# Seven block products of eight in the feed-forward's first product and in six of eight gated units of a conformer, with two accumulators in tiles of their own

## Chip, cores and metric

The kernel runs on one core of one Trainium2 chip. The metric is the device time of one execution in microseconds (us). All inputs and outputs are in HBM; the kernel starts with nothing on chip.

## The reference, cut to what matters

One residual block over 16 learned positions and 512 frames (T = 528), model width 1024, in float32. `hybrid_layer` reads, in short:

```
u = rmsnorm(h, norm_mix_w);  proj = u @ w_in                 # 1024 x 8208
c_val, c_gate, q, k, v, z, a_dt, b_beta, gate_logits = split(proj)
c = c_val * sigmoid(c_gate)                                   # the gated unit, 1024 channels
c = silu(layernorm(causal_dwconv(c, 31 taps)));  y_conf = c @ w_conf_out
o = gated delta rule over q, k, v (8 heads of 128, chunks);  y_dn = (rmsnorm(o) * silu(z)) @ w_dn_out
h = h + (sigmoid(gA) * y_conf + sigmoid(gB) * y_dn) @ w_out
up = causal_dwconv(rmsnorm(h, norm_ffn_w) @ w_up, 3 taps)     # 1024 x 5632: the feed-forward's first product
f_gate, f_val = split(up);  h = h + (silu(f_gate) * f_val) @ w_down
out = rmsnorm(h, norm_final_w), the 512 frames
```

## The kernel before

Activations lie transposed: 128 channels on the partitions, time along the free dimension, so a width of 1024 is 8 tiles. Every large product is made of three partial ones, because each operand is held as two float32r tiles, hi (the rounded value) and lo (what was left): hi times hi, hi times lo and lo times hi are added in PSUM. `weights` loads a 128 x 1024 block of a weight matrix on the SP queue into a tile `wr` (3 slots), ScalarE casts it to `wh` and VectorE subtracts to `wl` (2 slots each). `gemm` then issues, for one output tile of 128 channels, 8 blocks of the contraction x 3 parts x 2 halves of the time axis = 48 matmuls. The order of the parts is PARTS: the two with `wh` first, the one with `wl` last.

`glu(f)` (eight times) makes tile f of the gated unit from two such products, `cg` and `cv`, of 264 columns a matmul: tanh of half the gate on ScalarE, one VectorE instruction for the product, then the 31 taps of the depthwise convolution, 30 of them VectorE instructions into `ca`, which are given a late priority (+20000). Between and behind them come the keys, the heads of the delta rule (`heads`), the gates, the layer norm of `ca` and the three products behind it. `up(t)` (44 times) makes one tile of the feed-forward's first product, 258 columns a matmul, from the residual `hs` times its norm weight, as `hh` and `hl`; the factor of the second norm, `r2v`, is multiplied in when `up` takes the result out of PSUM, so that the products need not wait for it. Three taps follow (one on ScalarE, two on VectorE), Silu of the gate tile, the product of both, and a split into `fh`, `fl`. Then come 8 output tiles of the down product, `dn`, and the final norm.

Nothing is executed in the order of the source. `record` writes all instructions down with a priority, and `Plan.order` puts each engine's instructions into a fixed order by simulating the engines with costs of its own (`price`, `LAT`, RATE) and priorities shifted by BIAS, IVP, LNP and the like. On the chip each engine then runs its list in that order and waits on semaphores. SBUF tiles come from pools of fixed size: `bt` (128 x 532 float32) has 75 slots, which nearly all activations share, `iv` 3. In PSUM `p2` has 2 slots of two banks and `p1` 4 slots of one bank. All instructions are emitted by one line, so the profile's line is L459 nearly everywhere; groups are told apart by tile names.

POOL's queue holds the memsets of the first columns of `ra` (the padding that q, k and v are convolved with), eight `affine_select` for the decay tiles `E`, and four memsets of `LL`. All DMAs are issued on SP's queue.

## Time and profile before

| what | us |
|---|---|
| runs, median of 3 (lowest to highest) | 1035.56 (1034.06 to 1035.69) |
| the profiled execution's own time | 1031.66 |
| span of its trace, first to last instruction | 1029.9 |
| TensorE busy | 1015.1 |
| VectorE busy | 717.1 |
| ScalarE busy | 473.6 |
| GpSimd busy | 9.4 |

The profiled execution is one run; its own time is the span and 1.8 us around it. It lies 3.9 us below the median of the three runs. Busy times are of instructions on the engine; waits and DMA issues are not in them.

### The profile page before, as it was taken

The numbers are of one execution on the slowest core, as the hardware profiler recorded it, in microseconds if no ns is written. First come the engines' busy times: TensorE is split into PE (matmuls) and PEld (weight loads), VectorE is DVE, ScalarE is ACT, GpSimd is POOL, SyncE is SP. The second block draws the span as 40 slices with busy tenths as digits, with TensorE's granted clock in tenths as the row PEclk, the third lists the DMA queues.
The fourth block names the chain that finished last, engine by engine and source line by source line (L and its number), as shares of the span: only waits on it lengthen the run. The fifth ranks groups of instructions, "written<-read, shape, count | busy, mean of one in ns | idle before, by whom it ended". The sixth has DMA issues, their size and how long they took to land.

```text
span 1029.9 us, 20012 instructions
## 1 busy us (share of the span) xinstructions
PE 1015.1 (99%) x8430; PEld 973.8 (95%) x8430; DVE 717.1 (70%) x1237; ACT 473.6 (46%) x844; POOL 9.4 (1%) x45
## 2 busy tenths in 40 slices
PE   9998999999999999999999999999999999999996
PEld 7998999998999999999999999999999999988886
DVE  5987999999999999443565555666676767622334
ACT  6777713468545545444373334544434443422222
POOL 0000000000000000000000000000000000000000
PEclk9999999998999999999999999999999999999999
DMA  6243423241212133123214333222232222233332
GB/s 229 76 115 82 128 90 114 83 103 64 73 63 82 53 114 115 62 73 114 93 43 154 128 109 100 85 83 100 86 99 88 86 99 87 93 93 92 97 92 82
DMA packets 44042, 98.40 MB, mean 96 GB/s; under 512 B 12720, under 2 KB 19248, under 8 KB 43952
## 3 DMA queue, kind: packets, MB, share of 16 engines
q1 hardware_dynamic: 43952, 97.12, 29.5%
q8 instruction: 66, 1.08, 0.4%
q14 instruction: 24, 0.20, 0.1%
HBM read 93.89 MB, written 3.21 MB: 94 GB/s over the span
## 4 chain that ended last, share of the span: by engine, by line
PE 93%; DVE 4%; ACT 1%; DMA 1%; issue 0%; SPq 0%; DVEq 0%; ACTq 0%
PE up L459 25%; PE dn L459 12%; PE ga L459 9%; PE y L459 9%; PE q L459 5%; PE v L459 5%; PE z L459 5%; PE wo L459 5%; PE cv L459 4%; PE cg L459 4%; PE o L459 2%; DVE cv L459 1%; PE k L459 1%; PE rs L459 1%; PE S L459 1%; PE qk L459 1%
## 5 line engine op out<-in xcount | busy, mean ns | idle before, releaser
L459 DVE TENSOR_TENSOR wl<-wr,wh 128x1024 fp32r<-128x1024 f32 x157 | 189.2, 1206 | 154.3 <-PE dn L459 59.8
L459 ACT CAST wh<-wr 128x1024 fp32r<-128x1024 f32 x157 | 162.2, 1035 | 257.1 <-PE dn L459 58.2
L459 DVE SCALAR_TENSOR_TENSOR ca<-c,par,ca 128x516 f32<-128x516 f32 (+12 forms) x240 | 176.7, 745 | 3.7 <-ACT ca L459 1.0
L459 PE MATMUL up<-hl,wh 128*128 128x258 f32 x704 | 141.5, 282 | 0.0
L459 PE MATMUL up<-hh,wh 128*128 128x258 f32 x704 | 141.5, 282 | 0.0
L459 PEld LDWEIGHTS up<-hh,wh 128*128 128x128 f32 x704 | 109.2, 190 | 0.2 <-issue 0.2
L459 PEld LDWEIGHTS up<-hl,wh 128*128 128x128 f32 x704 | 108.7, 189 | 0.0
L459 PE MATMUL up<-hh,wl 128*128 128x258 f32 x704 | 92.3, 284 | 0.0
L459 PEld LDWEIGHTS up<-hh,wl 128*128 128x128 f32 x704 | 88.2, 190 | 0.0
L459 PE MATMUL dn<-fh,wh 128*128 128x512 f32 (+1 forms) x198 | 71.6, 370 | 0.0
L459 PE MATMUL dn<-fl,wh 128*128 128x512 f32 (+1 forms) x198 | 71.6, 370 | 0.0
L459 DVE SCALAR_TENSOR_TENSOR uy<-up,par,uy 128x512 f32<-128x512 f32 x88 | 65.9, 749 | 2.8 <-ACT uy L459 1.3
L459 DVE TENSOR_TENSOR up<-up,r 128x258 f32<-128x258 f32 x88 | 33.5, 420 | 47.4 <-PE up L459 44.6
L459 ACT ACTIVATE uy<-up,par 128x512 f32<-128x512 f32 x44 | 35.9, 817 | 55.8 <-DVE up L459 55.8
L459 PE MATMUL ga<-ul,wh 128*128 128x258 f32 (+1 forms) x256 | 58.0, 288 | 0.0
L459 PE MATMUL ga<-uh,wh 128*128 128x258 f32 (+1 forms) x256 | 57.2, 288 | 0.0
L459 DVE SCALAR_TENSOR_TENSOR cv<-ra,par,cv 128x528 f32<-128x528 f32 x69 | 51.7, 765 | 1.4 <-ACT cv L459 1.3
L459 PE MATMUL dn<-fh,wl 128*128 128x512 f32 (+1 forms) x198 | 45.4, 369 | 0.0
L459 PEld LDWEIGHTS dn<-fh,wh 128*128 128x128 f32 x198 | 37.2, 188 | 7.0
L459 PEld LDWEIGHTS dn<-fl,wh 128*128 128x128 f32 x198 | 37.2, 188 | 6.9
L459 PE MATMUL ga<-uh,wl 128*128 128x258 f32 (+1 forms) x256 | 43.1, 286 | 0.0
L459 PEld LDWEIGHTS ga<-ul,wh 128*128 128x128 f32 x256 | 42.2, 190 | 0.6 <-issue 0.4
(284 smaller groups left out, 2194.6 us busy)
## 6 DMA issues: line engine op xcount, KB each, us to landing
wr<-in_win SPq DMA_DIRECT2D x64, 512.0 KB, 3.4
wr<-in_wup SPq DMA_DIRECT2D x44, 512.0 KB, 3.4
wr<-in_wd SPq DMA_DIRECT2D x17, 512.0 KB, 3.5
wr<-in_wdn SPq DMA_DIRECT2D x8, 512.0 KB, 3.5
wr<-in_wco SPq DMA_DIRECT2D x8, 512.0 KB
wr<-in_wo SPq DMA_DIRECT2D x8, 512.0 KB, 3.4
wr<-in_wd SPq DMA_DIRECT2D x8, 384.0 KB, 3.5
x<-in_xT SPq DMA_DIRECT2D x8, 264.0 KB, 5.6
```

The costliest lines, as they stand in the source:

```text
L459: getattr(engines[o.eng], o.fn)(*(get(x) for x in o.a), **{n: get(x) for n, x in o.k.items()})
```

## The change

The first product of the feed-forward is taken in pairs, a gate tile with its value tile (22 pairs). The first NPRE = 3 pairs stay as they were. The other 19, and six of the eight gated units (all but the first NGLU = 2), become products of 2 x 2 blocks: the contraction is cut into even and odd tiles of 128, the output into the two tiles of the pair, and the time axis into its two halves. Seven block products (12 matmuls each: 4 blocks of the contraction x 3 parts) replace eight.

- `seven` runs the seven products into two PSUM tiles of one bank, X and Z, of pool `p1`, by turns X, Z, X, Z, X, Z, X. A product in X or Z goes on adding to what is there, and `use` reads the running sum after each product: four times on ScalarE (copy, or times -1), three times on VectorE (added to or subtracted from the copy in SBUF). `quarters` says which quarter of the two result tiles each reading goes to.
- The weights need seven blocks of 128 x 512 for a pair: three are plain, four are sums or differences. `presums` makes these four ahead, in DRAM, with DMAs issued on POOL's queue that add while they copy: five DMAs for a pair, those for the gated units after the load of x, those for the feed-forward after the last `affine_select`. Each group also waits for the one two before it. `seven` then calls `weights` four times, three times for 1024 columns and once for 512.
- The activations need seven blocks too. `ufactors` makes them for the gated units from `us`, once for each two tiles of the contraction; `factors` does it for the feed-forward, from the normalised residual, which `second_norm` now computes itself (16 instructions).
- For the 19 pairs the norm's factor is no longer multiplied in when PSUM is read. The taps are split off as `taps3` and `ends`, under a priority of their own.
- The residual tiles `hs` are written to DRAM (`d_h`) and read back tile by tile in the down product (`back`). `fh`, `fl` of the last three pairs go to slots of pool `iv`.
- The 32 diagonal copies into `Mn` move from ScalarE to POOL.
- The order's constants change (RATE, STAY, SWITCH, IVP, `tail`, a price for DMAs of POOL, and the table BIAS, which is left out below).

```diff
-RATE = 0.4453
+RATE = 0.4475
...
-STAY = 1500
-SWITCH = 300
...
+STAY = 7500
+SWITCH = 480
...
-IVP = 1265
+IVP = 765
...
+NGLU = 2
+NPRE = 3
...
-        o.tail = 950 + (2800 if fn == "dma_start" and o.lat > 700 and self.run(k) <= P else 0)
+        o.tail = 1300 + (5000 if fn == "dma_start" and o.lat > 700 and self.run(k) <= P else 0)
...
+            if eng == "POOL":
+                return 1000, int(np.prod(out.shape)) * 4 / 122.0
...
+                dma = max(dma, t + 1350) + o.lat * (1.5 if soft > t else 1)
                 o.end = dma + o.tail
+            elif o.fn == "dma_start":
+                soft = max(soft, t + 2000) + o.lat
...
+    def presums(src, n, hold):
+        r = [plan.tile("dram", "con", [P, 4, HD], F32, "ws") for _ in range(n)]
+        for m in range(n):
+          with plan.at(1):
+            h = {hold} | ({softs[-2]} if len(softs) > 1 else set())
+            plan.after = set(h)
+            G.dma_start(out=r[m][:, 0:2], in_=src[:, m, 0:3:2])
+            plan.after = set(h)
+            G.dma_start(out=r[m][:, 2:4], in_=src[:, m, 0:2])
+            G.dma_start(out=r[m][:, 1:3], in_=src[:, m, 3:4].broadcast_to([P, 2, HD]), accum_op=ALU.add)
+            G.dma_start(out=r[m][:, 0], in_=r[m][:, 1], accum_op=ALU.add)
+            G.dma_start(out=r[m][:, 3], in_=r[m][:, 0], accum_op=ALU.add)
+            softs.append(len(plan.ops) - 1)
+        return r
...
+    def seven(src, m, sums, B, w, use):
+        X, Z = p1("sx")[:, :w], p1("sz")[:, :w]
+        flat = lambda v: v.rearrange("p b c -> p (b c)")
+        tiles = (flat(src[:, m, 0:2]), flat(sums[m][:, 0:2]), flat(sums[m][:, 2:4]), src[:, m, 2])
+        for i, (b, to, first, what) in enumerate((('b11', X, True, 'p1'), ('b21', Z, True, 'c11b'),
+                                                  ('t2', X, False, 'u2'), ('t1', Z, True, 'c22b'),
+                                                  ('t3', X, False, 'u3'), ('b22', Z, False, 'c12b'),
+                                                  ('t4', X, False, 'c21'))):
+            if i % 2 == 0:
+                with plan.at("sw"):
+                    hi, lo = weights(tiles[i // 2], D if i < 6 else HD)
+            n, c = len(B), i % 2 * HD
+            runs = [(k, x, y) for part in PARTS for k in range(n) for x, y in ((lo, 0), (hi, 0), (hi, 1))[part]]
+            for j, (k, x, y) in enumerate(runs):
+                PE.matmul(to, lhsT=x[:, c + k * P:c + (k + 1) * P], rhs=B[k][b][y], start=first and j == 0, stop=j == len(runs) - 1,
+                          skip_group_check=not first)
+            use(what, to)
...
+    def quarters(src, m, sums, B, w, n):
+        c = [bt(n=n), bt(n=n)]
+        q = lambda i, j: c[i][:, j * w:(j + 1) * w]
+        def use(what, acc):
+            i, j = {'p1': (0, 0), 'u2': (0, 1), 'c22b': (1, 1), 'c21': (1, 0),
+                    'c11b': (0, 0), 'c12b': (0, 1), 'u3': (1, 1)}[what]
+            if what in ('p1', 'u2'):
+                S.copy(out=q(i, j), in_=acc)
+            elif what in ('c22b', 'c21'):
+                S.mul(out=q(i, j), in_=acc, mul=-1.0)
+            else:
+                V.tensor_tensor(out=q(i, j), in0=q(i, j), in1=acc, op=ALU.subtract if i else ALU.add)
+        seven(src, m, sums, B, w, use)
+        return c
...
+    def factors(x0, x1, w, n, hold=None):
+        q = 2 * (w + 2)
+        sub = lambda t: t[:, :q].rearrange("p (b w) -> p b w", b=2)[:, :, :w]
+        two = lambda t: t[:, :2 * w].rearrange("p (b w) -> p b w", b=2)
+        t = bt(n=n + "t")
+        X0, X1, TT = two(x0), two(x1), two(t)
+        hold = set() if hold is None else {hold}
+        plan.after = set(hold)
+        V.tensor_tensor(out=TT[:, 0], in0=X0[:, 0], in1=X0[:, 1], op=ALU.subtract)
+        V.tensor_tensor(out=X0[:, 1], in0=X1[:, 1], in1=X0[:, 1], op=ALU.subtract)
+        V.scalar_tensor_tensor(out=TT[:, 1], in0=TT[:, 0], scalar=-1.0, in1=X1[:, 1], op0=ALU.mult, op1=ALU.subtract)
+        t4 = bt(n=n + "q")
+        V.scalar_tensor_tensor(out=t4[:, :w], in0=TT[:, 1], scalar=-1.0, in1=X1[:, 0], op0=ALU.mult, op1=ALU.subtract)
+        r = {}
+        for v, names in ((X0, ('b11', 't3')), (X1, ('b21', 'b22')), (TT, ('t1', 't2'))):
+            hi, lo = bt(F32R, n + "h"), bt(F32R, n + "l")
+            plan.after = set(hold)
+            S.copy(out=sub(hi), in_=v)
+            V.tensor_tensor(out=sub(lo), in0=v, in1=sub(hi.bitcast(F32)), op=ALU.subtract)
+            for b, nm in enumerate(names):
+                r[nm] = (sub(hi)[:, b], sub(lo)[:, b])
+        hl = bt(F32R, n + "hl")
+        S.copy(out=sub(hl)[:, 0], in_=t4[:, :w])
+        V.tensor_tensor(out=sub(hl)[:, 1], in0=t4[:, :w], in1=sub(hl.bitcast(F32))[:, 0], op=ALU.subtract)
+        r['t4'] = (sub(hl)[:, 0], sub(hl)[:, 1])
...
+    def ufactors(k):
+        two = lambda t: t[:, :T].rearrange("p (b w) -> p b w", b=2)
+        X0, X1 = two(us[k]), two(us[k + 1])
+        t, q = bt(n="ut"), bt(n="uq")
+        TT, QQ = two(t), two(q)
+        V.tensor_tensor(out=TT[:, 0], in0=X0[:, 0], in1=X0[:, 1], op=ALU.subtract)
+        V.tensor_tensor(out=QQ[:, 0], in0=X1[:, 1], in1=X0[:, 1], op=ALU.subtract)
+        V.scalar_tensor_tensor(out=TT[:, 1], in0=TT[:, 0], scalar=-1.0, in1=X1[:, 1], op0=ALU.mult, op1=ALU.subtract)
+        V.scalar_tensor_tensor(out=QQ[:, 1], in0=TT[:, 1], scalar=-1.0, in1=X1[:, 0], op0=ALU.mult, op1=ALU.subtract)
+        r = {}
+        for v, names in ((t, ('t1', 't2')), (q, ('t3', 't4'))):
+            hi, lo = split(v[:, :T], T, "uf")
+            for b, nm in enumerate(names):
+                r[nm] = (two(hi)[:, b], two(lo)[:, b])
+        for nm, j, b in (('b11', 0, 0), ('b21', 1, 0), ('b22', 1, 1)):
+            c = slice(PAD + 264 * b, PAD + 264 * (b + 1))
+            r[nm] = (uh[k + j][:, c], ul[k + j][:, c])
+        return r
...
+    wgs, uf = presums(A['wgq'], KT - NGLU, max(j for x in xh for _, j, w in x.tl.hist if w)), []
...
-                S.copy(out=Mn[h][r, :, r], in_=D8(h)[r])
+                G.tensor_copy(out=Mn[h][r, :, r], in_=D8(h)[r])
...
+        if f < NGLU:
+            acc = p2("cg")
+            gemm(acc, weights(A['win'][8 + f]), uh, ul, FULL)
+            t = bt(n="ct")
+            S.activation(out=halves(t[:, :T], 264), in_=acc[:, :, :264], func=AF.Tanh, scale=0.5)
+            acc = p2("cv")
+            gemm(acc, weights(A['win'][f]), uh, ul, FULL)
+            c = bt(n="c")
+            V.scalar_tensor_tensor(out=halves(c[:, :T], 264), in0=halves(t[:, :T], 264), scalar=1.0, in1=acc[:, :, :264],
+                                   op0=ALU.add, op1=ALU.mult)
+        else:
+            t, c = quarters(A['wgq'], f - NGLU, wgs, uf, 264, "c")
+            S.activation(out=t[:, :T], in_=t[:, :T], func=AF.Tanh, scale=0.5)
+            V.scalar_tensor_tensor(out=c[:, :T], in0=t[:, :T], scalar=1.0, in1=c[:, :T], op0=ALU.add, op1=ALU.mult)
...
+    for k in range(0, KT, 2):
+        with plan.at("gf"):
+            uf.append(ufactors(k))
...
+    wus = presums(A['wuq'], FT - NPRE, masks[-1])
...
+    d_h = [con([P, SEQ], "d_h", "dram") for _ in range(KT)]
+    for f in range(KT):
+        SY.dma_start(out=d_h[f], in_=hs[f][:, 4:TW])
...
+        for f in range(0, KT, 2):
+            with plan.at(f"h{f}"):
+                ab = []
+                for i in range(2):
+                    x = bt(n="xn")
+                    for b in range(2):
+                        V.scalar_tensor_tensor(out=x[:, b * 258:(b + 1) * 258], in0=hs[f + i][:, 2 + 256 * b:260 + 256 * b],
+                                               scalar=pc('nf', f + i), in1=r2v[b], op0=ALU.mult, op1=ALU.mult)
+                    ab.append(x)
+                ub.append(factors(*ab, 258, "n"))
...
+    def ffn(t):
+        if t < NPRE:
+            g, v = up(t), up(NPRE + t)
+        else:
+            g, v = quarters(A['wuq'], t - NPRE, wus, ub, 258, "up")
+        with plan.at("tp" if t < NPRE else "tq"):
+            ends(t, g, v)
+    def ends(t, g, v):
+        g = taps3(g, t)
         S.activation(out=g[:, :SEQ], in_=g[:, :SEQ], func=AF.Silu)
-        v = up(FT + t)
+        v = taps3(v, FT + t)
         V.tensor_tensor(out=g[:, :SEQ], in0=g[:, :SEQ], in1=v[:, :SEQ], op=ALU.mult)
-        a, b = split(g[:, :SEQ], SEQ, "f")
+        if t < FT - 3:
+            a, b = split(g[:, :SEQ], SEQ, "f")
+        else:
+            hl = plan.tile("sb", "iv", [P, D], F32R, "fv")
+            a, b = hl[:, :SEQ], hl[:, SEQ:]
+            S.copy(out=a, in_=g[:, :SEQ])
+            V.tensor_tensor(out=b, in0=g[:, :SEQ], in1=a.bitcast(F32), op=ALU.subtract)
         fh.append(a)
         fl.append(b)
+    for t in range(FT):
+        call(ffn, "u", t)
...
+    def back(f):
+        o = bt(n="hr")
+        SY.dma_start(out=o[:, 4:TW], in_=d_h[f])
+        hr.append(o)
+        return o
...
-        o = hs[f]
+        o = back(f)
...
+def _quarters(w):
+    k, n = w.shape
+    v = w.reshape(k // 256, 2, P, n // 256, 2, P).transpose(2, 3, 4, 1, 0, 5)
+    v = np.stack([v[:, :, 0, 0], v[:, :, 0, 1], v[:, :, 1, 1], v[:, :, 1, 0]], 2)
+    return np.ascontiguousarray(v).reshape(P, n // 256, 4, k // 2)
...
+    glu = np.stack([w[:, D:2 * D].reshape(D, KT, P), w[:, :D].reshape(D, KT, P)], 2)
+    a['wgq'] = _quarters(glu[:, NGLU:].reshape(D, -1))
...
+    w = w_up[0].reshape(D, 2, FT, P)
+    a['wup'] = _pack(w[:, :, :NPRE].reshape(D, -1))
+    a['wuq'] = _quarters(w[:, :, NPRE:].transpose(0, 2, 1, 3).reshape(D, -1))
+    a['wd'] = _pack(w_down[0])
```

## Rows read from the trace of the kernel before

**Rows 1.** The page: span, busy time by engine, VectorE's busy tenths in 40 slices.

```profile
span 1029.9 us, 20012 instructions
PE 1015.1 (99%) x8430; PEld 973.8 (95%) x8430; DVE 717.1 (70%) x1237; ACT 473.6 (46%) x844; POOL 9.4 (1%) x45
...
DVE  5987999999999999443565555666676767622334
```

**Rows 2.** The chain that ended last, shares of the span by engine.

```profile
PE 93%; DVE 4%; ACT 1%; DMA 1%; issue 0%; SPq 0%; DVEq 0%; ACTq 0%
```

**Rows 3.** Windows: length, busy us (instructions) by engine, clock, DMA share, GB/s.

```profile
70.00:180.00 110.00, 106.53 (x869) 104.08 (x868) 101.18 (x264) 56.52 (x160) 6.16 (x10) 1.00 0.38 112
180.00:425.00 245.00, 244.18 (x2352) 236.80 (x2351) 228.26 (x370) 133.62 (x287) 2.29 (x18) 0.99 0.26 81
425.00:640.00 215.00, 214.94 (x1890) 212.16 (x1890) 112.15 (x149) 90.59 (x135) 0.00 (x0) 1.00 0.30 100
...
640.00:674.40 34.40, 34.40 (x292) 34.04 (x291) 23.05 (x34) 16.78 (x22) 0.00 (x0) 1.00 0.26 85
...
725.00:875.00 150.00, 150.00 (x1253) 150.00 (x1252) 103.06 (x157) 62.02 (x78) 0.00 (x0) 1.00 0.28 92
...
894.80:1018.00 123.20, 123.20 (x615) 102.20 (x614) 42.72 (x53) 35.43 (x43) 0.00 (x0) 1.00 0.29 86
```

**Rows 4.** The chain in order of time: start us, us, what.

```profile
127.73 5.85 PE cv L459 x48
...
639.82 5.97 PE up L459 x49
...
650.35 244.47 PE up L459 x2037
...
894.82 115.13 PE dn L459 x528
```

**Rows 5.** Groups of instructions in 675:875: busy us, mean ns, idle before.

```profile
L459 DVE SCALAR_TENSOR_TENSOR uy<-up,par,uy 128x512 f32<-128x512 f32 x70 | 52.4, 749 | 1.2
L459 DVE TENSOR_TENSOR wl<-wr,wh 128x1024 fp32r<-128x1024 f32 x35 | 42.5, 1215 | 0.0
L459 ACT CAST wh<-wr 128x1024 fp32r<-128x1024 f32 x35 | 36.4, 1039 | 38.3 <-PE up L459 38.3
L459 ACT ACTIVATE uy<-up,par 128x512 f32<-128x512 f32 x35 | 28.6, 817 | 47.8 <-DVE up L459 47.8
L459 DVE TENSOR_TENSOR up<-up,r 128x258 f32<-128x258 f32 x70 | 26.5, 420 | 38.0 <-PE up L459 38.0
L459 DVE TENSOR_TENSOR fl<-uy,fh 128x512 fp32r<-128x512 f32 x17 | 11.8, 692 | 23.7 <-ACT fh L459 23.7
```

**Rows 6.** ScalarE and VectorE in order of time where the second norm's factor arrives.

```profile
649.94 0.82 ACT L459 COPY r<-rc 128x258 f32<-128x258 f32 x2 [3.27 <-PE rc L459]
...
650.80 0.76 DVE L459 TENSOR_TENSOR up<-up,r 128x258 f32<-128x258 f32 x2 [2.81 <-ACT r L459]
```

**Rows 7.** Tile `ca`: durations (min/median/max ns), first and last start.

```profile
L459 DVE SCALAR_TENSOR_TENSOR ca<-c,par,ca x240: 706/746/1147, 95.0 to 412.0; 128x516 f32<-128x516 f32 x46, 128x515 f32<-128x515 f32 x8, 128x513 f32<-128x513 f32 x8, 128x511 f32<-128x511 f32 x8
...
L459 DVE TENSOR_TENSOR ca<-ca,mean x8: 687/690/695, 517.3 to 521.6; 128x516 f32<-128x516 f32 x8
```

**Rows 8.** POOL and VectorE in order of time: start us, us, what [idle before].

```profile
71.83 1.11 POOL L459 TENSOR_SCALAR_AFFINE_SELECT E<-E 128x512 f32<-128x512 f32 x1 [64.31 <-DMA E<-d_g]
...
75.11 0.63 POOL L459 TENSOR_SCALAR_AFFINE_SELECT E<-E 128x512 f32<-128x512 f32 x1 [2.17 <-DMA E<-d_g]
...
113.11 0.14 POOL L459 MEMSET ra<- 128x4 f32 x2
...
397.92 0.17 POOL L459 MEMSET ra<- 128x4 f32 x3 [41.30 <-ACT v L459]
...
72.36 1.13 DVE L459 SCALAR_TENSOR_TENSOR cv<-ra,par,cv 128x528 f32<-128x528 f32 x1
```

**Rows 9.** DMA: the queue with its share of 16 engines; issues with median us to landing.

```profile
q1 hardware_dynamic: 43952, 97.12, 29.5%
...
wr<-in_wup SPq DMA_DIRECT2D x44, 512.0 KB, 3.4
...
x<-in_xT SPq DMA_DIRECT2D x8, 264.0 KB, 5.6
```

More of the change, by code (lines that the diff above doesn't have):

```diff
@@ L37 @@
 ROW = T + PAD
+HD = D // 2
 _COLS = [('mix', 8), ('cw', 8 * KCONF), ('cb', 8), ('lw', 8), ('lb', 8), ('dw', 24 * 4), ('bg', 16),
@@ L63, in __init__ @@
         self.row = int(np.prod(shape[1:]))
-        self.hist, self.first, self.real, self.left = [], None, None, 0
+        self.hist, self.first, self.real, self.left, self.serial = [], None, None, 0, plan.count
 class Vw:
@@ L242, in at @@
         was = self.late
-        self.prio, self.late = self.prio + by, was or late and by > 0
+        self.prio, self.late = self.prio + by, was or late
         yield
@@ L333, in order @@
         for v in {v for o in ops for v in o.tiles if v.tag in KEEP}:
-            heapq.heappush(line[v.tag], (v.first, id(v), v))
-        table, dma, low, done = None, 0.0, 0, bytearray(len(ops))
+            heapq.heappush(line[v.tag], (v.first, v.serial, v))
+        table, dma, soft, low, done = None, 0.0, 0.0, 0, bytearray(len(ops))
         array = Array()
@@ L420, in order @@
             if e == "SP":
-                dma = max(dma, t + 1350) + o.lat
+                dma = max(dma, t + 1350) + o.lat * (1.5 if soft > t else 1)
                 o.end = dma + o.tail
+            elif o.fn == "dma_start":
+                soft = max(soft, t + 2000) + o.lat
+                o.end = soft + 1500
             out.append(i)
@@ new lines, in ufactors @@
+    def ufactors(k):
[15 more added lines that the diff above has]
+            r[nm] = (uh[k + j][:, c], ul[k + j][:, c])
+        return r
@@ L642, in record @@
     raw = [out_raw(acc) for acc in raw]
+    softs = []
+    wgs, uf = presums(A['wgq'], KT - NGLU, max(j for x in xh for _, j, w in x.tl.hist if w)), []
     us = []
@@ L797, in decays @@
                         compare_op=ALU.is_ge, fill=-1e30)
+        masks.append(len(plan.ops) - 1)
         for n in range(NC):
@@ L845, in grams @@
             SY.dma_start(out=d_m[b, h].rearrange("n j t -> j n t"), in_=mn[32 * b:32 * b + 32, :, 32 * b:32 * b + 32])
+    masks = []
     ivt = {}
@@ L959, in glu @@
     def glu(f):
-        acc = p2("cg")
-        gemm(acc, weights(A['win'][8 + f]), uh, ul, FULL)
-        t = bt(n="ct")
-        S.activation(out=halves(t[:, :T], 264), in_=acc[:, :, :264], func=AF.Tanh, scale=0.5)
-        acc = p2("cv")
-        gemm(acc, weights(A['win'][f]), uh, ul, FULL)
-        c = bt(n="c")
-        V.scalar_tensor_tensor(out=halves(c[:, :T], 264), in0=halves(t[:, :T], 264), scalar=1.0, in1=acc[:, :, :264],
-                               op0=ALU.add, op1=ALU.mult)
+        if f < NGLU:
[12 more added lines that the diff above has]
+            V.scalar_tensor_tensor(out=c[:, :T], in0=t[:, :T], scalar=1.0, in1=c[:, :T], op0=ALU.add, op1=ALU.mult)
         a = bt(n="ca")
@@ L1197, in record @@
         sq = s
-    r2v = []
+    d_h = [con([P, SEQ], "d_h", "dram") for _ in range(KT)]
+    for f in range(KT):
+        SY.dma_start(out=d_h[f], in_=hs[f][:, 4:TW])
+    r2v, ub = [], []
     def second_norm():
@@ L1212, in up, with taps3 @@
         u = bt(n="up")
+        for b in range(2):
+            V.tensor_tensor(out=u[:, b * 258:(b + 1) * 258], in0=acc[:, b, :258], in1=r2v[b], op=ALU.mult)
+        return u
+    def taps3(u, t):
         uv = halves(u[:, :516], 258)
-        for b in range(2):
-            V.tensor_tensor(out=uv[:, b], in0=acc[:, b, :258], in1=r2v[b], op=ALU.mult)
         y = bt(n="uy")
@@ L1224, in record @@
     fh, fl = [], []
-    for t in range(FT):
-        g = up(t)
+    def ffn(t):
[7 more added lines that the diff above has]
+        g = taps3(g, t)
         S.activation(out=g[:, :SEQ], in_=g[:, :SEQ], func=AF.Silu)
-        v = up(FT + t)
+        v = taps3(v, FT + t)
         V.tensor_tensor(out=g[:, :SEQ], in0=g[:, :SEQ], in1=v[:, :SEQ], op=ALU.mult)
-        a, b = split(g[:, :SEQ], SEQ, "f")
+        if t < FT - 3:
[5 more added lines that the diff above has]
+            V.tensor_tensor(out=b, in0=g[:, :SEQ], in1=a.bitcast(F32), op=ALU.subtract)
         fh.append(a)
         fl.append(b)
+    for t in range(FT):
+        call(ffn, "u", t)
     cuts = ((0, 8), (8, 8), (16, 6))
+    hr = []
+    def back(f):
[3 more added lines that the diff above has]
+        return o
     def wdown(f, i):
@@ L1253, in record @@
     f, hw, ws = KT - 1, SEQ // 2, {}
-    o, s = hs[f], bt(n="fsq")
+    o, s = back(f), bt(n="fsq")
     for b in range(2):
@@ L1272, in record @@
             for j in range(2):
-                V.tensor_tensor(out=y[:, j], in0=hs[i + j][:, ch], in1=rb[:, :hw], op=ALU.mult)
+                V.tensor_tensor(out=y[:, j], in0=hr[i + j][:, ch], in1=rb[:, :hw], op=ALU.mult)
             SY.dma_start(out=out[i:i + 2, :, c].rearrange("f p t -> p f t"), in_=y)
@@ L1320, in arrays @@
     a['wco'], a['wdn'], a['wo'] = _pack(w_conf_out[0]), _pack(w_dn_out[0]), _pack(w_out[0])
-    a['wup'], a['wd'] = _pack(w_up[0]), _pack(w_down[0])
+    w = w_up[0].reshape(D, 2, FT, P)
+    a['wup'] = _pack(w[:, :, :NPRE].reshape(D, -1))
+    a['wuq'] = _quarters(w[:, :, NPRE:].transpose(0, 2, 1, 3).reshape(D, -1))
+    a['wd'] = _pack(w_down[0])
     taps = lambda v: v.reshape(v.shape[0], -1, P).transpose(2, 1, 0).reshape(P, -1)
```

2 lines of the change are left out of this document (1 added, 1 removed).

## The prediction, as put on record before the result

> **What bounds the kernel now.** I read the page first: TensorE is busy for 1015.1 of 1029.9 us, VectorE for 70%, ScalarE for 46%, GpSimd for 1% [rows 1]. A busy TensorE alone proves nothing, so the chain of waits came next: 93% of it is TensorE, 4% VectorE, 1% each ScalarE and DMA [rows 2]. Then the windows by stage [rows 3]: from 425 us to the end of the down product TensorE never rests. From 70 to 425 it loses 3.5 and 0.8 us, and there VectorE is nearly full too: 101.2 of 110, then 228.3 of 245. So fewer matmuls shorten the kernel wherever something else does not take their place, and the reader is to see which engine has how much room: in the feed-forward VectorE is 103.1 of 150 us busy, ScalarE 62.0.
>
> **What it removes.** A pair of feed-forward tiles takes 96 matmuls of 258 columns; seven products of 12 take 84. In the chain 2037 such matmuls last 244.47 us, 120.0 ns each [rows 4], so a pair goes from 11.52 to 10.08 us. 19 pairs x 12 x 0.120 = 27.4 us. A gated unit has 264 columns, 48 matmuls in 5.85 us or 121.9 ns [rows 4]: 6 x 12 x 0.1219 = 8.8 us. Together 36.2 us of TensorE's time. Each matmul already has a weight load of its own (8430 and 8430, [rows 1]), so that each block product meets new weights changes nothing.
>
> **What it adds on VectorE and ScalarE in the feed-forward.** Now a pair is 2 weight subtractions of 1.215, 4 readings of PSUM at 0.420, 4 taps at 0.749 and 2 of 0.692 (the product of gate and value taken as the split): 8.49 us by duration [rows 5]. The window has 103.06 us in 150/11.52 = 13.0 pairs, 7.92 each [rows 3]; instructions back to back overlap a little, factor 0.933. After: 3.5 subtractions and 3 readings, so 8.49 + 1.82 - 0.42 = 9.89, times 0.933 = 9.2 of 10.08 us, 92%. ScalarE has 62.02/13.0 = 4.8 us; it gains 1.5 casts of 1.039 and 4 readings, as the 258-column copy, whose two take 0.82 together with their overlap [rows 6], or 0.41 each: 4.8 + 1.6 + 1.6 = 8.0, 79%. Both still fit, VectorE only just. What it cannot do in time are taps, which nothing reads before the down product.
>
> **Waits that it adds.** X may not be written before its running sum has been read. While it is read the product in Z runs, 12 x 0.120 = 1.44 us; the reading is 0.41 or 0.42. It is late only when its engine has just begun something long: 1.215 + 0.42 is 0.2 us over 1.44. Five such waits in a pair, 25 pairs. Bounds: nothing, or 125 x 0.2 = 25 us. I take one wait in six, 4 us, because VectorE is full at 92% but the order puts the reading by its priority.
>
> **Weights.** A pair needs 3.5 tiles, one in 2.88 us instead of 5.76. A `wr` slot is held for landing, cast and subtraction, 3.4 + 1.04 + 1.22 + an issue of 0.3 = 6.0 us [rows 5, 9]; three slots give one in 2.0 us. Even the slowest landing in the rows, 5.6 us, gives 2.7. In the two `wh`, `wl` slots a tile has 2.88 us for 1.04 + 1.22 = 2.26. Hidden, with 0.6 us to spare; if that is gone it shows as a wait behind ScalarE or VectorE, counted above. The load in the feed-forward rises from 92 GB/s, 0.28 of the DMA engines [rows 3], to 1.835 MB in 10.08 us, 182 GB/s and about 0.55. The 16 transfers of `d_h` carry 4 MB beside 97 [rows 9] and are read one tile per 15 us of down product; nothing.
>
> **Entry to the feed-forward.** The first product starts at 639.8 [rows 4] and the norm's factor is there at 650.8 [rows 6]. Three plain pairs last 34.6 us, so 23.6 are left for 16 normalising instructions and four calls of `factors` (each 4 of half width, 3 at full width and one more of half width). By the nearest rows, 0.42 and 0.69, that is 6.7 + 8.4 + 8.3 = 23.4 us of VectorE, beside 5.0 for readings and 7.3 for six weight tiles: 35.7 x 0.933 = 33.3. At most 9.7 us too much, at least nothing: the first product needs only 12.9 us of the 23.4. I take 4. The taps of three pairs, 13.1 us, are pushed back; 19 pairs with 0.85 us to spare each give 16. If some is left at the end, the first 16 contraction tiles of two `dn` results cover it: 96 matmuls of 0.218 [rows 4] are 21 us. I take 1 for this.
>
> **The stretch from 70 to 425 us.** Each of six gated units adds 1.5 subtractions and 3 readings (3.1 us) to VectorE, `ufactors` four times 4 half and 2 full instructions (3.1 us): 18.6 + 12.3 = 31, some 29 with the overlap. VectorE has about 26 us of room here, but 240 of its instructions are taps into `ca` of 0.746 that have the last priority: they end at about 412, and the layer norm subtracts at 517.3 [rows 7], 105 us later. Between 425 and 640 VectorE is half idle [rows 3]. So the 29 us move taps to 441 and are hidden. Not hidden is what the new tiles take: `ufactors` keeps 16 more of the 75 `bt` slots while gated units are unfinished, and the result tiles wait there for their taps. What is late next is work of TensorE whose result has no slot. Bounds: nothing, or the whole 29 us. I take 5, as if the 4.3 us lost here now doubled. The changed constants of the order lie inside this.
>
> **POOL.** Five DMAs for each of 25 pairs go into a queue that holds almost nothing now. Behind a waiting DMA stand the memsets of `ra`, for which the convolutions of q and v wait, and the moved diagonal copies; the last memset runs at 397.9 [rows 8]. The feed-forward's sums start when the last select is done, near 113, and are first read after 670: they have over 500 us. No row shows a DMA on POOL. From below: 2 MB for a pair at the hardware queue's 97.12 MB in 29.5% of 1029.9 us (320 GB/s) is 6.6 us; from above: four dependent steps at 5.6 and that, 29 us. The order is written as if it were 122 GB/s, 17.2 us; this is no time of the chip, but it fixes how closely the queue is packed. Between 6.6 and 29 I take the middle, near 17, at which the order holds, and a cost of nothing. The Trainium skill, page "DMA: Bandwidth & Descriptors", section "Anatomy of one DMA — SWDGE (gpsimd) path", gives about 2.0 us plus bytes/436 GB/s for a DMA from POOL. That would make (as an estimate) two 512 KB copies and sums of 512, 256 and 256 KB some 12 to 15 us; no run so far shows it, and the sum would stay as it is.
>
> A select takes 0.63 us at 75.11 but 1.11 at 71.83, and a VectorE instruction that began within it took 1.13, where its kind takes 0.75 [rows 5, 8]. So the 32 copies moved to POOL may cost VectorE some 0.4 us each, 12 us among taps that can be late. The Trainium skill, "SBUF — State Buffer", section "Who interferes with whom", has GpSimd and VectorE share one port pair, held for a whole instruction; the trace agrees with the 1.11 and 1.13 above.
>
> **Sum.** -36.2 + 4 (readings) + 4 (entry) + 1 (taps at the end) + 5 (the long stretch) = -22. The profiled execution has 1031.7, so 1009.5 on its scale; it lies 3.9 below the median of the runs, and on theirs I predict 1013 us.
>
> **The rivals.** (1) Everything hides: only -36 + 3, 1002.6. For it: all added work lies on engines with room; against it: VectorE at 92%. (2) VectorE bounds the feed-forward: in order and with waits it does not keep up, and a pair takes 10.9 us instead of 10.08 (9.89 plus five waits of 0.2). 19 x 0.82 = 15.6 us are given back, less the 3 of the 4 for readings that fall here: 1026. For it: TensorE waits for VectorE and ScalarE in turn, and each waits for TensorE; against it: 30% of VectorE's work is taps with time. (3) Slower: the chained DMAs take longer than the order assumes, and POOL's queue falls behind. From 113 to 398 us, 285/17.2 = 16.6 pairs stand before the last memset. At a fifth more, 3.4 us each, POOL is 57 us late; the heads' convolutions wait, TensorE with them, less some 10 us of slack: about 1060. It decides from about a tenth above 17.2, where the lag passes 32 us. For it: the strict queue and no row on such a DMA; against it: the lower bound of 6.6 us. (4) The gain is used up by slots and entry together: 1035.
>
> **Chances.** Forecast 0.60, (1) 0.14, (2) 0.13, (3) 0.10, (4) 0.03. Three runs here differ by 0.16%, so 0.2% is about what can be told from no change. Faster: 0.60 + 0.14 + 0.13 = 0.87; same 0.03; slower 0.10. The range 1001 to 1028 takes in the forecast, (2) and nearly all of (1); with (3), (4) and tails of (1) and (2) outside, a fifth is left out. The forecast's own range is 1005 to 1021.
>
> **What would show it.** Right: TensorE's instructions fall by 300 (25 x 12); 258-column matmuls still come every 120 ns; VectorE is near 92% in the feed-forward, and a pair takes 10.1 to 10.4 us; POOL's last memset is still near 400. Wrong: a pair of 11 us with TensorE waiting for VectorE (2); memsets of `ra` late behind DMAs and TensorE idle between 113 and 425 (3); a lower granted clock after pauses; weights landing after 6 us or more.

## The result, and the profile after

The changed kernel takes 1049.85 us (median of four runs, 1047.90 to 1052.85) against 1034.81 us for the kernel before on the same chip: 1.0148 times as long, 95% interval 1.0128 to 1.0168. The forecast was 1013 us, its range 1001 to 1028. The profiled execution has a span of 1048.4 us, 18.5 more than before.

The page of the changed kernel, the parts that answer to [rows 1, 2, 9]:

```profile
span 1048.4 us, 20173 instructions
...
PE 1002.5 (96%) x8130; PEld 952.5 (91%) x8130; DVE 791.6 (76%) x1358; ACT 543.7 (52%) x984; POOL 129.8 (12%) x202
...
PE   8999678899999999999999999998999999999996
...
PEclk8999888899999999999999999999999999999998
DMA  9957698897788888798641235422656565733332
...
q1 hardware_dynamic: 53456, 120.98, 36.5%
q0 software_dynamic: 21200, 52.44, 25.6%
...
PE 80%; DVE 10%; DMA 6%; ACT 3%; issue 1%; SPq 0%; DVEq 0%; ACTq 0%
```

TensorE executes exactly the 300 matmuls less that were forecast, and its busy time falls by 12.6 us; the span grows all the same, because it now rests, and runs at the lower of its two clock levels behind such rests. The fifth slice (105 to 131 us) has a 6, and the clock is 8 there. The row of the DMA engines shows why to look further: 7 to 9 in nearly every slice up to 500 us, where the stretches before had 0.26 to 0.38 [rows 3]. DMA has 6% of the chain instead of 1%.

The stages, from the first instruction of a tile to that of the next (gate product `cg`, first `q`, first `up`, first `dn`, end), in us of span; the third column is an experiment that is told below:

| stage | before | after | without POOL's DMAs |
|---|---|---|---|
| start to `cg` | 70.2 | 79.5 | 71.0 |
| gated stretch, `cg` to `q` | 110.3 | 139.2 | 118.4 |
| heads to `up` | 459.0 | 458.3 | 456.2 |
| feed-forward's first product | 255.0 | 235.7 | 234.6 |
| `dn` to the end | 135.4 | 135.7 | 134.5 |

The feed-forward gains 19.3 us. The start loses 9.3 and the gated stretch 28.9, although 8.8 us of matmuls are gone from it. The windows of the changed kernel, columns as in [rows 3]:

```profile
0.00:25.00 25.00, 19.80 (x112) 13.06 (x114) 13.30 (x38) 11.75 (x17) 5.27 (x19) 0.80 0.95 315
...
125.00:180.00 55.00, 39.87 (x255) 37.33 (x255) 39.33 (x111) 19.72 (x35) 12.17 (x15) 0.84 0.84 194
180.00:225.00 45.00, 41.68 (x306) 41.06 (x305) 38.87 (x85) 18.97 (x31) 7.60 (x11) 0.89 0.86 231
225.00:425.00 200.00, 199.05 (x2000) 191.96 (x1999) 184.10 (x294) 110.03 (x224) 62.62 (x102) 1.00 0.84 194
...
680.00:725.00 45.00, 43.01 (x353) 41.67 (x352) 40.19 (x80) 26.62 (x41) 0.00 (x0) 1.00 0.30 92
725.00:775.00 50.00, 47.50 (x383) 46.50 (x384) 48.36 (x72) 37.90 (x61) 0.00 (x0) 1.00 0.52 164
775.00:875.00 100.00, 100.00 (x830) 99.86 (x829) 90.90 (x129) 73.28 (x119) 0.00 (x0) 1.00 0.59 185
```

From 125 to 180 us TensorE and VectorE are both idle for more than a quarter of the time: neither bounds this stretch. The chain of the changed kernel names who does, start us, us, what:

```profile
3.09 12.15 DMA x<-in_xT
...
134.28 4.88 DMA d_mm<-Mm
...
139.23 6.75 DMA iv<-d_mm
...
147.23 9.40 DMA wr<-in_wgq
...
168.98 9.47 DMA wr<-in_wgq
...
187.16 9.58 DMA wr<-ws
```

Loads of x and of weights stand on the path. These three weight loads take 9.4 to 9.6 us where one took 3.4 in the median, and the load of x takes 12.15 where it took 5.6 [rows 9]. Just ahead of them the chain has two transfers of 8 KB for the inverses, `d_mm` and `iv`; in the run without sums, below, no DMA stands on the chain of the gated stretch. And POOL's row in order of time shows that its DMAs run beside x from the beginning:

```profile
1.45 1.58 POOL L471 DMA_DIRECT2D ws<-in_wgq  x2 [0.20 <-issue]
3.00 0.14 POOL L471 MEMSET ra<- 128x4 f32 x1
3.04 1.09 POOL L471 DMA_DIRECT2D ws<-in_wgq  x2
```

`presums` gives its DMAs a `hold`, the last writer of `xh`. It is used only where the order of the instructions is simulated. On the chip nothing waits: no data joins these DMAs to x, and POOL had little else in its list. The same holds for the wait of each group for the one two before it: it stands in the simulated order alone, and on the chip a DMA of POOL waits only for the data that it reads or adds to, and for its turn.

### The profile page after: what moved, and what is told of

It reads as the page before. It is cut to its first block, busy times and chain, and to the rows that moved or that the text cites. A ratio compares the mean times of both kernels' runs of the same rounds, so it can differ in the third digit from the quotient of the medians.

```text
span 1048.4 us, 20173 instructions
## 1 busy us (share of the span) xinstructions
PE 1002.5 (96%) x8130; PEld 952.5 (91%) x8130; DVE 791.6 (76%) x1358; ACT 543.7 (52%) x984; POOL 129.8 (12%) x202
## 3 DMA queue, kind: packets, MB, share of 16 engines
q0 software_dynamic: 21200, 52.44, 25.6%
## 4 chain that ended last, share of the span: by engine, by line
PE 80%; DVE 10%; DMA 6%; ACT 3%; issue 1%; SPq 0%; DVEq 0%; ACTq 0%
PE dn L471 12%; PE sx L471 11%; PE y L471 9%; PE ga L471 8%; PE sz L471 8%; PE q L471 5%; PE wo L471 4%; PE v L471 4%; PE z L471 4%; DVE wl L471 2%; PE k L471 2%; DMA wr<-in_wgq 2%; PE o L471 2%; DMA wr<-ws 1%; DVE cv L471 1%; DMA x<-in_xT 1%
## 5 line engine op out<-in xcount | busy, mean ns | idle before, releaser
L471 DVE TENSOR_TENSOR wl<-wr,wh 128x1024 fp32r<-128x1024 f32 (+2 forms) x207 | 237.0, 1146 | 147.1 <-PE dn L471 60.2
L471 ACT CAST wh<-wr 128x1024 fp32r<-128x1024 f32 (+2 forms) x207 | 204.2, 987 | 233.5 <-PE dn L471 60.1
L471 POOL DMA_DIRECT2D ws<-in_wuq x57 | 48.8, 872 | 146.2 <-issue 72.3
L471 POOL DMA_DIRECT2D ws<-ws x50 | 46.4, 928 | 124.2 <-DMA ws<-ws 61.8
L471 PE MATMUL sx<-nh,wh 128*128 128x258 f32 x228 | 57.7, 284 | 2.5 <-ACT up L471 2.5
L471 PE MATMUL sz<-nl,wh 128*128 128x258 f32 x228 | 57.5, 283 | 0.6 <-DVE nl L471 0.6
L471 PE MATMUL sz<-nh,wh 128*128 128x258 f32 x228 | 57.6, 284 | 0.2
L471 PE MATMUL sx<-nl,wh 128*128 128x258 f32 x228 | 57.6, 284 | 0.0
L471 PEld LDWEIGHTS sx<-nh,wh 128*128 128x128 f32 x228 | 43.2, 189 | 3.1 <-ACT up L471 3.1
L471 PEld LDWEIGHTS sz<-nl,wh 128*128 128x128 f32 x228 | 43.2, 190 | 0.8 <-DVE nl L471 0.8
```

The costliest lines, as they stand in the source:

```text
L471: getattr(engines[o.eng], o.fn)(*(get(x) for x in o.a), **{n: get(x) for n, x in o.k.items()})
```

## The experiments

Times are medians; before on the same chip was 1033.5 to 1034.4 us. Set against each other were: the bytes of POOL's DMAs slow the loads (theory 1); the changed order and the block form itself (theory 2); POOL's queue with its waits, the third rival's mechanism (theory 3); the added work on VectorE, tested by its block activations (theory 4). A fifth, the order of the grams, came up in the course; it is not the "Rival 5" that the text on record for the run without block activations names.

**Without the sums.** The order stays; POOL's DMAs are not issued, and plain blocks are read where the sums were.

```diff
+        for m in range(n):
+            r[m].tl.real = src.make()[:, m]
...
+                if o.eng == "POOL" and o.fn == "dma_start":
+                    continue
```

> The changed kernel with its order of instructions as it is, but the 125 DMAs on POOL's queue are left out and the products read plain weight blocks of the same size in place of the sums (the result is not the reference's). Theory 1 (the DMAs of POOL share the DMA engines, weight tiles land after 9.5 us instead of 3.4, and the block form, which uses up a tile in 2.9 us, cannot hide that): the first gated product starts near 70 us instead of 79.5, heads start near 175 to 185 instead of 218.7, the time is 1008 to 1018. Theory 2 (the block form itself costs it: readings of the accumulators, tile slots, the changed order): 1042 to 1050. Theory 3 (POOL's queue is late with its selects and memsets): as theory 1, 1008 to 1018.

1018.09 us, 0.9858 (0.9840 to 0.9876), span 1014.7: at the upper edge of what theories 1 and 3 gave, and the heads start at 189.4, later than the 175 to 185 expected. The stages are in the table above: the DMAs cost 33.7 us in all, 8.5 at the start, 20.8 in the gated stretch, 2.1 in the heads, 2.3 behind. So most of the loss goes with the DMAs, whatever in them it is. But the gated stretch still takes 8.1 us more than before.

**Small sums.** All 125 DMAs with the waits that their data give them, each with a sixteenth of its bytes; nobody reads them.

```diff
+                    cut = lambda r: r[:, :, :32] if len(r.shape) == 3 else r[:, :32]
+                    k = {n: cut(get(x)) if n in ("out", "in_") else x for n, x in o.k.items()}
+                    engines["POOL"].dma_start(**k)
+                    continue
```

> As the run without sums, but the 125 DMAs stay on POOL's queue with all their waits, each moving a sixteenth of its bytes to where nobody reads it (not the reference's result). Theory 1 (bytes on the DMA engines): within 6 us of the run without sums, 1008 to 1022. Theory 3 (the queue's waits): at least half of the loss stays, 1030 to 1048, with selects as late as in the changed kernel. Theory 2: 1042 to 1050.

1020.14 us, 0.9874 (0.9859 to 0.9889). The page of this kernel, POOL's own busy time and its DMA queue:

```profile
PE 990.8 (97%) x8130; PEld 944.8 (93%) x8130; DVE 790.2 (78%) x1358; ACT 542.8 (53%) x984; POOL 135.6 (13%) x202
...
q0 software_dynamic: 15600, 3.28, 4.3%
```

POOL is as busy as in the changed kernel (135.6 against 129.8), its instructions are the same, and by the medians the loss is gone within 2 us. So it goes with the bytes, 3.28 MB instead of 52.44. Fewer bytes shorten the waits in POOL's own queue too (the last `ra` memset comes at 406.0 instead of 445.0), so this run alone does not part theory 1 from theory 3. The trace of the changed kernel does: none of POOL's instructions is on its chain, and in its list of waits no other engine waits for one of them. Theory 3 falls for the changed kernel.

**Idle sums.** The kernel before, with the 125 DMAs beside it, their results unread.

```diff
+    presums(A['wgq'], KT - NGLU, max(j for x in xh for _, j, w in x.tl.hist if w))
...
+    presums(A['wuq'], FT - NPRE, masks[-1])
```

> The kernel before, all products in their old form, with the 125 DMAs of the changed kernel added on POOL's queue; nobody reads the sums. Theory 1: a weight tile feeds 5.85 us there, so landing after 9 us is hidden (12 us a slot in three slots is one in 4.0 us); only the start, where x lands late, costs 6 to 10 us: 1040 to 1046, TensorE busy above 99% from 100 to 425 us. Theory 3: memsets and selects wait, 1055 or more. Theory 2: 1035 to 1038.

1073.05 us, 1.0383 (1.0351 to 1.0416): for theory 1 a miss by 27 us and more, and a time that theory 3 had allowed (1055 or more). The old form loses 7.8 us at the start, 14.0 in the gated stretch and 20.7 in the heads. Its windows:

```profile
185.00:225.00 40.00, 40.00 (x330) 39.47 (x329) 39.71 (x85) 15.94 (x24) 11.08 (x18) 1.00 0.95 230
225.00:275.00 50.00, 41.59 (x522) 39.86 (x523) 42.73 (x73) 26.47 (x67) 11.89 (x16) 0.82 0.85 199
```

The old form, which wants half as many bytes a second, was expected to suffer less. In the gated stretch it does, 14.0 us against 20.8; in the heads it loses 20.7, where the changed kernel loses 2.1. Waits for POOL do not explain it: ScalarE waits 4.2 us for POOL's selects in all (2.0 in the kernel before), and TensorE never waits for POOL. In the chain from 233 us on stand the transfers of the inverses, `d_x` with 5.76 us and `DU` with 11.23, a landing that took 4.7 before. That the changed kernel's order is spared because it counts on slow transfers is a guess, not tested here.

**A hold on the chip.** POOL copies one column of the last x before its first DMA, and waits for it.

```diff
+    held = con([P, 1], "held")
+    G.tensor_copy(out=held, in_=xs[-1][:, :1])
```

> The changed kernel with a copy of one column of the last x tile on POOL ahead of the first sums, so that its queue really waits until x has landed. Theory 1: x lands as in the kernel before (first products of x near 8 us instead of 15), the first plain gated product comes some 6 to 9 us earlier, but the sums for the gated units come 10 to 15 us later than now and the gated stretch still crawls: 1040 to 1050. Theory 2: 1042 to 1050, with no change but the start. Theory 3: slower, 1052 or more, as the whole queue starts later.

1039.19 us, 1.0063 (1.0048 to 1.0078), 0.8 below the range of theory 1. In its chain x is there much sooner, and weights stay late:

```profile
3.08 6.00 DMA x<-in_xT
...
146.59 9.18 DMA wr<-in_wgq
```

The start takes 71.9 us, 7.6 less; the gated stretch 138.1, nearly as long as it was.

**Each part alone.** First the feed-forward in block form, the gated units and the order's constants as before:

```diff
-NGLU = 2
+NGLU = 8
...
-    wgs, uf = presums(A['wgq'], KT - NGLU, max(j for x in xh for _, j, w in x.tl.hist if w)), []
+    wgs, uf = [], []
```

> Feed-forward in block form alone: all eight gated units in their old form, no sums and no block activations for them, order constants of the kernel before (with the changed kernel's for the new parts), diagonal copies back on ScalarE. The sums for the feed-forward start when the selects are done, near 115 us. Theory 1 (bytes of POOL's DMAs against the weight loads): the feed-forward gives its 19 us, and the sums, which lie beside the inverses' small transfers and the heads as in the run with idle sums, take back 8 to 20: 1024 to 1036. Theory 2 (the gated units' block form is what costs, with or without DMAs): 1012 to 1018.

1023.69 us, 0.9902 (0.9878 to 0.9926), at the lower edge of theory 1's range: it beats both kernels. Then the gated units alone, with the hold on x:

```diff
-NPRE = 3
+NPRE = 22
...
-    wus = presums(A['wuq'], FT - NPRE, masks[-1])
+    wus = []
```

> The gated units alone in block form, with the hold on x; the feed-forward in its old form, no sums for it. Theory 1: the gated units' own sums (12.6 MB) lie beside the keys' weights and the first gated units, so the stretch from the first gated product to the heads is 120 to 126 us against 110 before, and with the spill of the residual 1042 to 1050, slower than the kernel before. Rival: with the feed-forward's sums gone the 8.8 us of saved matmuls come through, 1027 to 1035.

1054.42 us, 1.0201 (1.0177 to 1.0225), 4 us above the expected range. The gated stretch takes 126.6 us with 6 of the 25 groups of sums, 12.6 MB; the feed-forward lost 8 us here behind its entry. From 660 to 680 TensorE is busy for 16.34 of 20 us at a clock of 0.83: at the second norm it waits 2.31 us for `rr` and 1.35 us for the first reading of `up`, both on VectorE, and starts matmuls of 258 columns 0.21 us apart behind them. Why the order has nothing to put there is open; without these 8 us the run would lie in its range.

**Later sums.** The feed-forward's sums wait on the chip until the second call of `grow`; first in the kernel with the hold, where they start at 245 us, then in the one with the feed-forward alone, where they start at 233.

```diff
+            kept = con([P, 1], "kept")
+            G.tensor_copy(out=kept, in_=Mn[H - 1][:, 0, :1])
+            wus = presums(A['wuq'], FT - NPRE, len(plan.ops) - 1)
```

> The changed kernel with the hold on x and with the sums for the feed-forward held on the chip until the second merge of the inverses is done, near 260 us, so that only the sums for the gated units lie beside the gated units. Theory 1: the gated stretch shortens from 138 us by 10 to 15, the rest stays: 1024 to 1031, and the feed-forward does not wait for its sums (19 pairs at 20 us end near 640). Theory 2: 1036 to 1041.

1035.79 us, 1.0022 (0.9997 to 1.0048), with single runs from 1031.5 to 1042.1: 4.8 us above the expected range. The gated stretch fell by 13.0 us to 125.1, as expected, but the heads gave 6.6 back.

> Feed-forward in block form alone, with its sums held until the second merge of the inverses is done. Theory 1: nothing of POOL's moves before 250 us; the heads behind it take 0 to 5 us more: 1013 to 1021, the fastest so far that computes the reference. Theory 2: as feed-forward alone with early sums, 1012 to 1018 for both.

1024.22 us, 0.9907 (0.9884 to 0.9930): a miss, no better than with early sums. The heads take 476.3 us. A third try took the order's assumed delay of a transfer from before (`o.tail`: 950 and 2800 in place of 1300 and 5000):

> Feed-forward alone with late sums, the order's DMA tail set back to the kernel before's (950 and 2800 ns instead of 1300 and 5000). If the pause near 230 us (TensorE waits 3.6 us for a transpose, then runs at a lower clock) comes from an order that expects the inverses' transfers later than they land: TensorE above 49 of 50 us in 225:275 and 1016 to 1020. If the pause has another cause: 1021 to 1026.

1023.47 us, 0.9908 (0.9884 to 0.9933). Windows of these two kernels, first with the new, then with the old delay:

```profile
225.00:275.00 50.00, 45.83 (x620) 43.20 (x613) 45.49 (x69) 30.82 (x78) 12.09 (x20) 0.80 0.67 154
...
475.00:525.00 50.00, 48.57 (x424) 47.82 (x423) 20.54 (x26) 18.17 (x26) 13.26 (x17) 1.00 0.95 225
```

```profile
225.00:275.00 50.00, 48.09 (x648) 45.64 (x639) 47.47 (x75) 33.51 (x84) 13.02 (x20) 0.93 0.78 184
...
475.00:525.00 50.00, 45.39 (x348) 44.48 (x347) 19.22 (x23) 12.87 (x16) 12.71 (x16) 0.93 0.90 198
```

The order's assumed delay is not the cause: the time stays, and the pause went to another place. Wherever the sums are put before the feed-forward, they cost about the same: without them (next) this kernel is 8.7 us faster.

**The block forms undisturbed.** The kernel with the feed-forward alone, its sums left out as in the first experiment:

> The run before this one (feed-forward alone, late sums) with the DMAs on POOL left out and plain blocks read in place of the sums (not the reference's result). Both theories: the feed-forward's 19 us and nothing else, 1012 to 1016. Against the changed kernel without sums (1018.1) it tells what the six gated units in block form are worth when no DMA disturbs them: if this run is faster, they cost more than the 8.8 us of matmuls that they save.

1015.54 us, 0.9822 (0.9798 to 0.9845). This is no slower than the same with gated units in block form too (1018.09), though these take 8.8 us of matmuls away. Gated stretch and heads together last 574.8 us here, 574.6 there, and 569.3 in the kernel before. So in these orders the block form of the gated units gains nothing even without DMAs. The two runs differ in the order's constants too, and the 5.5 us lost here, in the old form, go with a pause of their own: from 225 to 275 TensorE is busy for 45.85 of 50 us at a clock of 0.80, and it waits 3.6 us for `LL` on VectorE. The kernel with late sums has the same pause (the first of its windows above), so that one is not the work of the DMAs. To see whether VectorE is the cause in the gated stretch (theory 4), the gated units' block activations were not made and plain halves read:

```diff
     def ufactors(k):
-        two = lambda t: t[:, :T].rearrange("p (b w) -> p b w", b=2)
...
+        for i, nm in enumerate(('b11', 'b21', 't2', 't1', 't3', 'b22', 't4')):
+            c = slice(PAD + 264 * (i // 2 % 2), PAD + 264 * (i // 2 % 2 + 1))
+            r[nm] = (uh[k + i % 2][:, c], ul[k + i % 2][:, c])
```

> The changed kernel without sums, and also without the instructions that make the block activations of the gated units (the products read plain halves of the activations instead, so the result is not the reference's); everything else in the same order. Theory 4 (without DMAs the gated stretch is still long because these 16 VectorE and 8 casting or subtracting instructions, some 12 us of VectorE, stand in a queue that is already full ahead of the weight subtractions): the stretch from the first gated product to the heads falls from 118 us to 106 to 111, 1005 to 1011. Rival 5 (readings of the accumulators and weight tiles every 2.9 us): 115 to 119 us, 1014 to 1019.

1015.33 us, 0.9827 (0.9808 to 0.9845), the gated stretch 118.3 us against 118.4. Theory 4 falls for the block activations; the readings and the added weight tiles, on which the rival in that expectation puts the loss (115 to 119 us), were not taken out. TensorE in order of time, in the first experiment (no sums), start us, us, what, idle before it and what ended it:

```profile
107.99 0.28 PE L473 MATMUL ktm<-cst,cv 128*16 128x128 f32 x1 [3.42 <-ACT junk L473]
108.97 2.08 PE L473 MATMUL gg<-cv 128*128 128x128 f32 x8 [0.70 <-ACT kdm L473]
...
114.16 1.16 PE L473 MATMUL gg<-cv 128*128 128x128 f32 x8 [2.05 <-ACT kd L473]
...
121.55 0.59 PE L473 MATMUL sz<-uh,wh 128*128 128x264 f32 x1 [3.45 <-DVE mn L473]
```

These are 9.6 us of waits. The keys' grams `kt`, `ktm`, `gg` come in short pieces with ScalarE between them, and the products that could fill the gaps are used up: the two plain gated units end at about 103 us, and the block units' X and Z need slots of `p1`, which the grams hold (`sz` waits for the reading of a gram into `mn`). From 110 to 130 us the granted clock is 0.68, and TensorE is busy for 14.51 of 20 us; in the kernel before it is 1.00 and 19.94. This is theory 5. Four plain gated units instead of two, still without sums, should fill the gaps:

> The order without POOL's DMAs (the plain blocks are read in place of the sums, as in e1_no_sums), with NGLU = 4 in place of 2: four gated units are plain, four are block products. Against e1_no_sums TensorE gets 2 x 12 x 0.1219 = 2.9 us more to do. In e1_no_sums the stretch from the first gate product to the first q took 118.4 us, 8.1 more than the kernel before, although it has 8.8 us less of matmuls: 16.9 us are lost there. Theory 5 (the two plain units are used up before the last grams are done; X and Z then wait for slots of p1 that grams hold, and the clock falls in these pauses): two more plain units stand between the grams, the pauses between about 104 and 125 us go, and the stretch is 105 to 111 us; the kernel runs at 1006 to 1013. Its rival (each block unit loses the same by itself, 16.9/6 = 2.8 us, by its readings, weights or taps): the stretch is 110.3 - 5.9 + 11.3 = about 116, the kernel at 1014 to 1017. If the stretch stays above 117, neither holds.

1032.12 us, 0.9980 (0.9969 to 0.9990): a miss for both theories, by 15 us and more. The gated stretch takes 114.0 us, between what the two gave (111 and 116). The wait of `sz` is gone, but the first three are there as before (3.43, 0.70, 2.05): the last of these grams ends at 116.8 us, and the order put a whole block unit behind it and the first added plain one only at 129.3. So the edit put nothing more between the grams. And the heads take 476.2 us, 20 more than without this edit. VectorE of this kernel, in order of time:

```profile
308.24 6.95 DVE L473 SCALAR_TENSOR_TENSOR ca<-c,par,ca 128x506 f32<-128x506 f32 x9
315.10 0.60 DVE L473 SCALAR_TENSOR_TENSOR S<-S,cd,S 128x128 f32<-128x128 f32 x2
```

```profile
315.49 0.80 PE L473 MATMUL kS<-S,cv 128*128 128x128 f32 x2 [6.88 <-DVE S L473]
```

Nine taps into `ca`, which have time until 533, stand in VectorE's fixed list ahead of the update of the state S, for which TensorE waits 6.88 us; from 260 to 350 it rests 11.9 of 90 us, and the clock is 0.87 up to 300 and 0.90 behind. So theory 5 is not shown, and for the first three waits not tested. The wait of 3.4 us for the slot of `sz` went with the edit and the stretch is 4.4 us shorter, but by the rival's 116 fewer block units alone give 2.4 of that; that the other waits lengthen the stretch stays an argument. X and Z in slots of `p2` were not tried.

## Why the prediction was wrong, point by point

- **POOL, "a cost of nothing": wrong, by 33.7 us, and this alone turns the sign.** The step asked whether POOL's queue keeps up, and took the transfers for hidden because the sums have over 500 us. They have; the loads beside them have not. The bytes were added up for the feed-forward, and there rightly (0.59 of the DMA engines from 775 to 875, forecast 0.55); for 0 to 500 us, where 52.44 MB of sums are moved, they were not. The rows then available give the first half of that sum: 50 MB in some 500 us are 100 GB/s on top of 81 to 112. At the 320 GB/s that the step used for its lower bound this adds 0.31 to the loads' share of 0.26 to 0.38 [rows 3], some 0.57 to 0.69, not far from what the feed-forward bears. The other half was the price, which no row had: 25.6% of 1048.4 us for 52.44 MB is 195 GB/s at full share, against 316 for the hardware queue. At 195 the sums add 0.51, some 0.77 to 0.89, and 0.84 to 0.86 were measured from 125 to 425. Whether the DMA engines themselves or the memory behind them set that rate, no run here parts.
- **Weights: "Even the slowest landing in the rows, 5.6 us, gives 2.7".** That landing is one of x. For weights the rows that were read give a median, 3.4 us; the trace of before has longer ones, 6.6 us beside the loads of x in the first 25 us, and 9.3 between 65 and 70, beside four loads of `E` (DMA issues from 25 to 75 us; the last number is the median landing):

```profile
wr<-in_win SPq DMA_DIRECT2D x7, 512.0 KB, 9.3
E<-d_g SPq DMA_DIRECT2D x4, 256.0 KB
```

Three `wr` slots at 9.5 + 1.04 + 1.22 + 0.3 = 12.1 us give a tile in 4.0 us, where a block unit wants one in 2.9: as an estimate, for the 21 tiles of six units 1.1 us too much each, 23 us, near the 20.8 that the stretch lost to the DMAs. It takes every load as slow as the three on the chain and leaves out the 11.6 us of the two 8 KB transfers there; what share each had is not shown. The forecast's last line named "weights landing after 6 us or more" as what would show it wrong, and that is what the chain shows.
- **The hold of the first sums** was taken as the text has it, "after the load of x". It is a matter of the order, not of the chip: 7.6 us, given back by one copy.
- **"The stretch from 70 to 425 us, I take 5": too low.** Gated stretch and heads together should have come out 8.8 - 5 = 3.8 us shorter; without any sums they were 5.3 longer (574.6 against 569.3), 9.1 us off. The late step named, work of TensorE whose result has no slot, is seen in that run at `sz`, but in `p1`, among the grams, and not in `bt`. Of VectorE, on which the step spent its working, the block activations have no part in it; what the rest is stays open. With the sums 22.9 more are lost here.
- **The feed-forward: right in sum, with luck in the terms.** Forecast -27.4 + 4 + 4 + 1 = -18.4; measured -19.3, and +0.3 behind it. 830 matmuls recorded from 775 to 875 and not a moment of rest: a pair comes every 10.13 us (chain, `sx` at 789.78, 799.90, 810.03), forecast 10.08. So what the step says of the matmuls holds. VectorE is at 91% there (92), ScalarE at 73% (79). The readings cost nothing instead of 4 there. The entry cost 8 instead of 4 by the difference (235.7 - 227.6), of which the rows show 2.0 + 2.5 us of rest from 680 to 775, and 1.0 as pairs of 10.13; the other 2.6 have no row. The two errors of 4 us cancel.
- **The rivals.** (2) did not occur. (3) had the sign and the wrong mechanism: POOL's last `ra` memset is late (445.0 against 397.9, though the heads too start 38.2 us later), and the feed-forward's sums come every 19.9 us (141.6 to 519.1 for 19 pairs) instead of 17.2, above its point of decision; yet no other engine waits for an instruction of POOL, and the heads lose only 2.1 us to the DMAs. A row on POOL's DMAs was missing, as the prediction said; a doubtful price should have gone to every user of the same engines, not to one queue.

The Trainium skill, page "DMA: Bandwidth & Descriptors", section "Issuing engines are not separate DMA queues", says that transfers started from SP, ScalarE or GpSimd run on the same 16 engines and interleave. The two first experiments agree: 33.7 us with all the bytes, 2 with a sixteenth of them. It was the rule that spoke against this change, and the prediction cited another section of the page. That one, "Anatomy of one DMA — SWDGE (gpsimd) path", would make (as an estimate) 3.2 us of a 512 KB transfer; here they took 7.9 in the median, from DRAM to DRAM and beside the loads:

```profile
ws<-in_wuq POOLq DMA_DIRECT2D x57, 512.0 KB, 7.9
```

## What to carry to other kernels

Count the bytes of a background transfer against every load that shares the DMA engines in the same stretch, not only against its own due time, and give it a wait that exists on the chip. Test the parts of a large change one by one: the feed-forward alone beats both kernels here (1023.47 to 1024.22 us in three variants), while the gated units' block form gained nothing in the order tried here even without the sums' transfers. Where every engine has a fixed list, an edit far away reorders the rest by more than it saves (20 us between two orders of the same heads, 456.2 and 476.2 us, neither with a DMA of POOL), so compare stages, not totals, before a cause is named.

## What was not expected of the hardware

- Sums made by DMAs of POOL from DRAM to DRAM use the engines at 195 GB/s for full share, the loads at 316, and 512 KB weight loads beside them, the three on the chain, land after 9.4 to 9.6 us instead of 3.1 to 3.4.
- The 32 copies of 32 x 128 that moved to POOL take 18.6 us there (changed kernel, POOL in order of time: 8 in 6.08, 15 in 5.38, 9 in 7.17):

```profile
250.06 6.08 POOL L471 COPY mn<-DU 32x128 f32<-32x128 f32 x8 [11.22 <-DMA DU<-d_x]
...
257.94 5.38 POOL L471 COPY mn<-DU 32x128 f32<-32x128 f32 x15
...
264.46 7.17 POOL L471 COPY mn<-DU 32x128 f32<-32x128 f32 x9
```

- In the run without sums four waits of 0.70 to 3.45 us within 18 us went with a mean granted clock of 0.68 from 110 to 130 us, and matmuls of 264 columns started 0.22 us apart (`sx` from 115.92 on) in place of 0.122, as at the lower level, 1.2 GHz. A short rest of TensorE costs more than its own length.
